# Turning the outputs of a down projection: 32x32 blocks on VectorE and 128-byte stores in place of TensorE transposes

## The chip, the cores and the metric

The kernel runs on one core of a Trainium2 chip. The metric is the time of one execution on the device in microseconds, as the median of several runs. The engines are named as in the profile: PE is TensorE's matmul, PEld its weight load, DVE is VectorE, ACT is ScalarE, POOL is GpSimd, SP is SyncE, which here does nothing but put DMA transfers into its queue. Transfers that ACT or POOL put into a queue stand as ACTq and POOLq.

## The reference

One layer of an encoder: 512 new frames of one stream and 64 frames of another, 2048 channels, all in f32. The part that matters here is the last one, the feed-forward block with its residual:

```python
h2 = rmsnorm(x, g_norm2)
x = x + (jax.nn.silu(h2 @ w_gate) * (h2 @ w_up)) @ w_down
```

with `w_gate`, `w_up` of 2048 x 5632 and `w_down` of 5632 x 2048. It gives `y_prompt` (512 x 2048) and `y_sample` (64 x 2048), both with the token as the row. Ahead of it stand the attention heads, the gated convolution and their joint projection, which the change does not touch.

## The kernel before

All activations lie with the channel on the partition and the token in the free dimension. The 512 and 64 tokens are taken together as 576 (T) and cut into two halves of 288 (HALF, HALVES); so the second half holds 224 tokens of the prompt and the 64 of the sample.

Each f32 operand is split into two parts of a rounded type, `hi` and `lo`, and a product is three matmuls (hi x hi, lo x hi, hi x lo), line 1529. The large products are cut in 2 x 2 blocks of channels and tokens and made by a scheme of seven block products in place of eight: sums of weight blocks are made on DVE (lines 1471 to 1477), split by ACT (line 221) and DVE (line 222), and each product (`run`, with a number 1 to 7) adds into one, two or more of the four quarters of the result.

The down projection works on eight column blocks d of 256 output columns. The list DOWN says in which order the blocks are visited and over which pairs of hidden channels; an entry is a unit. The last eight units are the last visits of the eight blocks: blocks 0, 1, 3, 6 and 7 with five pairs each, block 5 with six, and then blocks 2 and 4 with four. In a unit of m pairs each of the seven runs has 3m matmuls of 128x288. The runs of neighbouring units are interleaved: run 1 of the next unit comes before runs 3 and 4 of this one.

A block's result has four quarters `acc[d, c, i]`, with c one of two groups of 128 columns and i one of the two halves of tokens; each is a tile of 128 channels x 288 tokens, into which DVE (line 1559) and POOL (line 1561) add. The last visit finishes them in the order (0, 0), (1, 1), (0, 1), (1, 0); in the very last unit (1, 0) comes before (0, 1). When a quarter is finished, `store_y` (line 1685) spawns its output work in a pipeline.

The pipeline (`Pipeline`, lines 66 to 91) counts ticks, one for each pair in a product, that is every three matmuls. A piece of work says with `yield n` that its next step shall be given out n ticks later. In the last part of the kernel ACT, DVE, SP, POOL and PE all take their instructions in the order in which the program gives them out, so a step's place in each engine's queue is set by its ticks.

The output work of a quarter before the change has three steps. After 9 ticks (4 in the last unit, `quick`) PE transposes two pieces of 128 tokens against an identity matrix into PSUM (line 1717), and, where a rest of 32 or 64 tokens is due, a third piece (line 1720). For blocks 4 and 5 (`lone`) each quarter has a rest of 32 tokens; for the others the two halves of a column group lie in one tile (`both`), and the second of them turns the rests of both, 64 tokens. Three ticks later ACT copies the result from PSUM back over the tile (line 1723), and the rest into a spare part of `raw_b` (line 1727). Four ticks later SP stores it: rows of 128 columns, so pieces of 512 bytes, in one transfer for the first half (line 1730), in up to three for the second (lines 1697 and 1699, as prompt and sample are two outputs), and one or two for the rest. In the last unit the rests go out by ACT's queue. In the last unit there are no ticks between the steps.

In the same queue of SP, in program order, stand the loads of the down projection's weights (`load_columns`, line 1415), each given out when the buffer that it fills has been read for the last time. The last two of them are issued at 2330 us. The loads of the hidden activations (lines 1678 and 1685) are in this queue too; the last of them come before the first store.

Of the kernel before, what the change touches and what calls it, by code (L numbers as in the profile page):

```python
# [16 lines left out]
P = 128  # L17
TP = 512
TS = 64
T = TP + TS  # L20
HALF = T // 2
# [73 lines left out]
def tile_hybrid_stream_step(  # L95
# [6 lines left out]
    nc = tc.nc  # L102
# [5 lines left out]
    yp, ys = y_prompt[0], y_sample[0]  # L108
# [52 lines left out]
    def weight_raw(i):  # L161
        src, nk, ncol = specs[i]
        raw = raw_tile["A"][:, i % 2, : nk * ncol]
        return raw, raw.rearrange("p (k c) -> p k c", k=nk), src
# [64 lines left out]
    ident = const.tile([P, P], F32, name="ident")  # L229
# [29 lines left out]
    def misc(name):  # L259
        return ps_z.tile([P, 512], F32, tag="misc", name=name, bufs=2)  # L260

    rows = {}
# [109 lines left out]
    with tc.manual_schedule(engines={mybir.EngineType.Activation, mybir.EngineType.DVE, mybir.EngineType.SP}):  # L372
        raw, raw3, src = weight_raw(0)
# [106 lines left out]
    t1 = tc.alloc_tile_pool(name="t1", bufs=1, reuse_waits="tile", side="left")  # L480
    dg = t1.tile([P, 5, P], F32, tag="vtok", name="dg")
    for i in range(5):
        n = P if i < 4 else TS
# [690 lines left out]
    for k_, (n, p_) in enumerate(corder):  # L1174
# [7 lines left out]
        if n == NCU - 1 and p_ in (6, 7, 4):  # L1182
            q = {6: 1, 7: 2, 4: 3}[p_]
            t = bt["pool"].tile([P, NH, 2, HALF], F32R, tag=f"t{q}", name=f"forms{q}")
# [244 lines left out]
    late = {}  # L1429
# [16 lines left out]
    NU = len(UNITS)  # L1446
# [86 lines left out]
    def run(n, p_):  # L1533
# [8 lines left out]
        def done(c, i, ps, part=None):  # L1542
            if kind != "down":
                finish(kind, fp, c, i, ps, part)
            elif n in last:
                store_y(n, c, i)
# [68 lines left out]
    for d, v in visits.items():  # L1615
        n = next(a for a, b in zip(v, v[1:]) if a >= NGU + 10 and b >= a + 4)
# [3 lines left out]
    both, one = {}, {}  # L1620
    down = {}
    turn = [0]
# [64 lines left out]
    def store_y(n, c, i):  # L1687

        d = UNITS[n][1]
        src, cs, f0 = acc[d, c, i], slice((2 * d + c) * P, (2 * d + c + 1) * P), HALVES[i][0]  # L1690
        r = HALF - 2 * P

        def put(f, ap, q=nc.sync):

            rows, n_p = ap.shape[0], max(min(TP - f, ap.shape[0]), 0)
            if n_p:
                q.dma_start(out=yp[f : f + n_p, cs], in_=ap[:n_p])
            if n_p < rows:
                q.dma_start(out=ys[f + n_p - TP : f + rows - TP, cs], in_=ap[n_p:])

        quick = n == NU - 1


        lone = (d, c) not in both
        k0 = 0 if lone or i == 0 else r
        rest = None
        if lone:
            rest = src[:, 2 * P :], f0 + 2 * P
        elif (d, c) in one:
            rest = both[d, c].rearrange("p i t -> p (i t)")[:, 2 * P : 2 * P + 2 * r], 2 * P  # L1710
        one[d, c] = i

        def work():
            yield 4 if quick else 9
            po = misc("pot")[:, : 3 * P]
            for q in range(2):
                nc.tensor.transpose(po[:, q * P : (q + 1) * P], src[:, k0 + q * P : k0 + (q + 1) * P], ident)
            if rest:
                nr = rest[0].shape[1]
                nc.tensor.transpose(po[:nr, 2 * P :], rest[0], ident)  # L1720
            yield 0 if quick else 3
            ob = src[:, k0 : k0 + 2 * P].rearrange("p (i c) -> p i c", c=P)
            nc.scalar.copy(out=ob, in_=po[:, : 2 * P].rearrange("p (i c) -> p i c", c=P))
            if rest:
                turn[0] += 1
                obs = late["raw"][: 2 * r, 4096 + turn[0] % 4 * P : 4096 + (turn[0] % 4 + 1) * P]
                nc.scalar.copy(out=obs[:nr], in_=po[:nr, 2 * P :])
            yield 0 if quick else 4
            if i == 0:
                nc.sync.dma_start(out=yp[: 2 * P, cs].rearrange("(i p) c -> p i c", p=P), in_=ob)  # L1730
            else:
                put(f0 + k0, ob[:, 0, :])
                put(f0 + k0 + P, ob[:, 1, :])
            if rest:
                put(rest[1], obs[:nr], nc.scalar if quick else nc.sync)

        pipe.spawn(work())


# [105 lines left out]
```

## Time and profile before

| What | Value |
|---|---|
| time, median of 3 runs | 2382.36 us (2382.0 to 2385.2) |
| span of the profiled execution | 2383.4 us |
| PE busy | 2361.4 us (99%) |
| DVE busy | 1919.3 us (81%) |
| ACT busy | 1172.1 us (49%) |
| POOL busy | 295.2 us (12%) |
| DMA packets | 512,260, 390.76 MB, of them under 512 bytes 11,838 |
| stores of y | 80 by SP, 4 by ACT |
| first and last transposes for the outputs | 2267.7 and 2378.9 us |

The profile comes from one execution, whose span is 1.0 us above the median of the runs. The page gives the busy time of each engine, the share of time in 40 slices, the DMA queues, and the chain of waits that ended last. A row of a timeline gives the start in us, the length in us, the engine, the line of the kernel, the operation, the tile written and the tile read, and the number of instructions that were merged. A row of a group gives line, engine, operation, tiles, shapes and count, then the busy time in us, the mean of one in ns, and the idle time before with what ended it. A row of one line's or one tile's instructions gives the count and the shortest, the median and the longest duration in ns, and when the first and the last of them started. The time of a DMA row on SP is the time that the queue spends on issuing it, not the transfer's.

### The profile page before, as it was taken

Reading aid. Unit: us, or ns where it says so; the run is one execution under the profiler, and the core shown is the slowest. Engines: PE = TensorE matmul, PEld = TensorE weight load, DVE = VectorE, ACT = ScalarE, POOL = GpSimd, SP = SyncE. Lnnn points to the kernel's source line nnn. Section 1 sums busy time; section 2 is a strip of 40 time slices with the busy share of each in tenths; the row PEclk is TensorE's granted clock in tenths of the full one; section 3 lists DMA queues with packets and bytes.
Section 4 is the critical chain, followed back from the end, with each engine's and each line's share of the span. In section 5 each row is a group of like instructions: output and inputs, shape, how many; then the busy total and the mean of one; then the engine's idle time right before and its main releaser. Section 6 shows DMA issues by size and latency. Waiting matters only on the chain.

```text
span 2383.4 us, 44109 instructions
## 1 busy us (share of the span) xinstructions
PE 2361.4 (99%) x17765; PEld 2349.5 (99%) x17765; DVE 1919.3 (81%) x2884; ACT 1172.1 (49%) x2107; POOL 295.2 (12%) x386
## 2 busy tenths in 40 slices
PE   8999999999999999999999999999999999999999
PEld 8999999999999999999999999999999999999999
DVE  7767776688887899888888888888888777887876
ACT  6666665444444555444444444444444444444444
POOL 1111111242111130000000000000000002431211
PEclk9999999999999999999999999999999999999999
DMA  8354433584367745444444444444444936886642
GB/s 257 117 152 142 144 112 96 184 285 127 109 216 199 217 155 177 151 125 147 152 131 143 150 137 140 147 144 134 146 147 133 355 116 207 221 231 198 202 132 81
DMA packets 512260, 390.76 MB, mean 164 GB/s; under 512 B 11838, under 2 KB 501176, under 8 KB 512056
## 3 DMA queue, kind: packets, MB, share of 16 engines
q1 hardware_dynamic: 502712, 371.40, 48.8%
q0 software_dynamic: 8624, 16.22, 3.3%
q8 instruction: 139, 2.28, 0.4%
q14 instruction: 65, 0.53, 0.1%
q10 hardware_dynamic: 720, 0.33, 0.0%
HBM read 298.82 MB, written 89.08 MB: 163 GB/s over the span
## 4 chain that ended last, share of the span: by engine, by line
PE 88%; DVE 5%; DMA 3%; ACT 2%; issue 1%; POOL 0%; SPq 0%; ACTq 0%; DVEq 0%; POOLq 0%
PE psy L1529 34%; PE psw L1529 17%; PE pj L212 11%; PE psx L1529 9%; PE psy L1033 5%; PE pjo L212 4%; PE psw L1033 3%; PE psx L1033 1%; DMA raw_a<-in_w_out_dram 1%; DMA o_ob<-xt_dram 1%; DVE whl L1005 1%; PE z L682 1%; PE po L749 0%; DMA raw_a<-in_w_down_dram 0%; DMA raw_a<-in_w_in_dram 0%
## 5 line engine op out<-in xcount | busy, mean ns | idle before, releaser
L1529 PE MATMUL psy<-h_s,whl 128*128 128x288 f32 x2787 | 411.4, 294 | 0.3 <-ACT part L1539 0.3
L212 PE MATMUL pj<-x,whi 128*128 128x288 f32 x1856 | 398.2, 299 | 0.3 <-DVE x L355 0.3
L1529 PEld LDWEIGHTS psy<-h_s,whl 128*128 128x128 f32 x2787 | 383.5, 188 | 0.6 <-ACT part L1539 0.6
L222 DVE TENSOR_TENSOR whl<-raw_a,whl 128x1024 fp32r<-128x1024 f32 (+4 forms) x296 | 323.1, 1092 | 59.1 <-ACT whl L221 58.3
L1529 PE MATMUL psw<-t,whl 128*128 128x288 f32 x2400 | 348.1, 295 | 0.0
L1529 PEld LDWEIGHTS psw<-t,whl 128*128 128x128 f32 x2400 | 327.7, 188 | 0.0
L221 ACT CAST whl<-raw_a 128x1024 fp32r<-128x1024 f32 (+4 forms) x296 | 267.8, 906 | 114.5 <-issue 35.4
L212 PEld LDWEIGHTS pj<-x,whi 128*128 128x128 f32 x1856 | 306.6, 189 | 1.0 <-DVE x L355 0.6
L212 PE MATMUL pj<-x,wlo 128*128 128x288 f32 x928 | 274.2, 295 | 0.1
L222 DVE TENSOR_TENSOR whl<-raw_b,whl 128x1024 fp32r<-128x1024 f32 (+5 forms) x190 | 200.6, 1056 | 70.4 <-ACT whl L221 69.2
L221 ACT CAST whl<-raw_b 128x1024 fp32r<-128x1024 f32 (+5 forms) x190 | 165.2, 872 | 169.1 <-issue 72.8
L1539 ACT COPY part<-psy 128x288 f32<-128x288 f32 x242 | 96.4, 398 | 282.8 <-PE psy L1529 281.3
L1529 PE MATMUL psy<-b22m,whl 128*128 128x288 f32 x1212 | 182.7, 294 | 0.4 <-ACT part L1539 0.4
L1529 PE MATMUL psy<-t2t,whl 128*128 128x288 f32 x1212 | 183.0, 294 | 0.0
L212 PEld LDWEIGHTS pj<-x,wlo 128*128 128x128 f32 x928 | 174.9, 188 | 0.7 <-DVE wlo L422 0.3
L1529 PE MATMUL psx<-h_s,whl 128*128 128x288 f32 x1185 | 173.5, 294 | 0.0
L1529 PEld LDWEIGHTS psy<-b22m,whl 128*128 128x128 f32 x1212 | 168.0, 188 | 0.7 <-ACT part L1539 0.7
L1529 PEld LDWEIGHTS psy<-t2t,whl 128*128 128x128 f32 x1212 | 168.2, 188 | 0.2 <-DVE whl L222 0.2
L1529 PEld LDWEIGHTS psx<-h_s,whl 128*128 128x128 f32 x1185 | 162.6, 188 | 0.0
L221 ACT CAST whl<-s 128x1024 fp32r<-128x1024 f32 (+5 forms) x81 | 72.3, 892 | 101.5 <-PE psw L1529 101.4
L1308 POOL DMA_DIRECT2D hid_dram<-form x3 | 2.2, 750 | 947.2 <-DVE form L222 947.2
L1529 PE MATMUL psy<-t,whl 128*128 128x288 f32 x576 | 107.6, 296 | 0.0
(483 smaller groups left out, 4446.7 us busy)
## 6 DMA issues: line engine op xcount, KB each, us to landing
hid_dram<-form SPq DMA_DIRECT2D x147, 288.0 KB, 2.3
raw_a<-in_w_in_dram SPq DMA_DIRECT2D x41, 1024.0 KB, 6.5
raw_a<-in_w_gate_dram SPq DMA_DIRECT2D x22, 1024.0 KB, 6.0
raw_a<-in_w_up_dram SPq DMA_DIRECT2D x22, 1024.0 KB, 5.7
raw_b<-in_w_gate_dram SPq DMA_DIRECT2D x22, 1024.0 KB, 6.6
raw_b<-in_w_up_dram SPq DMA_DIRECT2D x22, 1024.0 KB, 7.6
h_s<-hid_dram SPq DMA_DIRECT2D x10, 2016.0 KB, 11.6
raw_a<-in_w_out_dram SPq DMA_DIRECT2D x16, 1024.0 KB, 5.4
```

Source lines behind the costliest of these rows:

```text
L212: mm(ps, w_[:, k, csl], x_, start=(k == 0 and n == 0), stop=(k == nk - 1 and n == 2))
L221: nc.scalar.copy(out=hi, in_=src)
L222: (lo_eng or nc.vector).tensor_tensor(out=lo, in0=src, in1=hi.bitcast(F32), op=ALU.subtract)
L682: mm(zb[i], a_[:, kk], b_[:, q0:TP], start=(n == 0), stop=False, skip_group_check=True)
L1005: tt(out=whl[:, 1], in0=src, in1=whl[:, 0].bitcast(F32), op=ALU.subtract)
L1033: mm(ps, whl[:, w_, j, :], x_, start=(start and j == 0 and q == 0), stop=(j == m - 1 and q == 2), skip_group_check=True)
L1308: q.dma_start(out=hid_dram[fp][2 * n - 2 : 2 * n].rearrange("f p t -> p f t"), in_=t.bitcast(F32))
L1529: mm(ps, whl[:, w_, j, :], x_, start=(start and j == 0 and q == 0), stop=(j == len(xs_) - 1 and q == 2), skip_group_check=True)
L1539: nc.scalar.copy(out=t, in_=st["y"])
```

## The change

The transposes on PE, their copies on ACT and the rests are gone. When a quarter is finished, DVE turns its tile in place: each block of 32 channels x 32 tokens is transposed by itself, so that afterwards partition 32q + t holds, at 32b + c, what partition 32q + c held at 32b + t. That is, of the tokens 32b + t for all b, the 32 channels of group q lie next to one another. A store then takes 32 partitions (one q), and writes for each partition t and each block b a piece of 32 channels, 128 bytes, to the row of token 32b + t. Nine blocks make up a half of 288 tokens; the second half is cut at token 512, into seven blocks for the prompt and two for the sample. The first step comes 9 ticks after the quarter is finished (4 in the last unit), the stores 2 ticks later, all of them on SP's queue.

```diff
         d = UNITS[n][1]
         src, cs, f0 = acc[d, c, i], slice((2 * d + c) * P, (2 * d + c + 1) * P), HALVES[i][0]
-        r = HALF - 2 * P
-        def put(f, ap, q=nc.sync):
-            rows, n_p = ap.shape[0], max(min(TP - f, ap.shape[0]), 0)
-            if n_p:
-                q.dma_start(out=yp[f : f + n_p, cs], in_=ap[:n_p])
-            if n_p < rows:
-                q.dma_start(out=ys[f + n_p - TP : f + rows - TP, cs], in_=ap[n_p:])
...
+        def put(f, ap):
+
+            n_p = max(min(TP - f, HALF), 0)
+            for y, t0, t1, g in ((yp, 0, n_p, f), (ys, n_p, HALF, f + n_p - TP)):
+                if t1 > t0:
+                    for q in range(4):
+                        nc.sync.dma_start(
+                            out=y[g : g + t1 - t0, cs.start + 32 * q : cs.start + 32 * (q + 1)].rearrange("(b t) c -> t b c", t=32),
+                            in_=ap[32 * q : 32 * (q + 1), t0:t1].rearrange("t (b c) -> t b c", c=32))
         def work():
-            yield 4 if quick else 9
-            po = misc("pot")[:, : 3 * P]
-            for q in range(2):
-                nc.tensor.transpose(po[:, q * P : (q + 1) * P], src[:, k0 + q * P : k0 + (q + 1) * P], ident)
-            if rest:
-                nr = rest[0].shape[1]
-                nc.tensor.transpose(po[:nr, 2 * P :], rest[0], ident)
-            yield 0 if quick else 3
-            ob = src[:, k0 : k0 + 2 * P].rearrange("p (i c) -> p i c", c=P)
-            nc.scalar.copy(out=ob, in_=po[:, : 2 * P].rearrange("p (i c) -> p i c", c=P))
...
-            yield 0 if quick else 4
-            if i == 0:
-                nc.sync.dma_start(out=yp[: 2 * P, cs].rearrange("(i p) c -> p i c", p=P), in_=ob)
-            else:
-                put(f0 + k0, ob[:, 0, :])
-                put(f0 + k0 + P, ob[:, 1, :])
-            if rest:
-                put(rest[1], obs[:nr], nc.scalar if quick else nc.sync)
+
+            yield 4 if n == NU - 1 else 9
+            nc.vector.transpose(out=src, in_=src)
+            yield 2
+            put(f0, src)
 
         pipe.spawn(work())
```

More of the change, by code (lines that the diff above doesn't have):

```diff
@@ L1690, in store_y @@
         src, cs, f0 = acc[d, c, i], slice((2 * d + c) * P, (2 * d + c + 1) * P), HALVES[i][0]
-        r = HALF - 2 * P
-        def put(f, ap, q=nc.sync):
-            rows, n_p = ap.shape[0], max(min(TP - f, ap.shape[0]), 0)
-            if n_p:
-                q.dma_start(out=yp[f : f + n_p, cs], in_=ap[:n_p])
-            if n_p < rows:
[L1699 to L1711, printed above, removed]
-        def work():
-            yield 4 if quick else 9
-            po = misc("pot")[:, : 3 * P]
-            for q in range(2):
-                nc.tensor.transpose(po[:, q * P : (q + 1) * P], src[:, k0 + q * P : k0 + (q + 1) * P], ident)
-            if rest:
-                nr = rest[0].shape[1]
-                nc.tensor.transpose(po[:nr, 2 * P :], rest[0], ident)
-            yield 0 if quick else 3
-            ob = src[:, k0 : k0 + 2 * P].rearrange("p (i c) -> p i c", c=P)
-            nc.scalar.copy(out=ob, in_=po[:, : 2 * P].rearrange("p (i c) -> p i c", c=P))
-            if rest:
-                turn[0] += 1
-                obs = late["raw"][: 2 * r, 4096 + turn[0] % 4 * P : 4096 + (turn[0] % 4 + 1) * P]
-                nc.scalar.copy(out=obs[:nr], in_=po[:nr, 2 * P :])
-            yield 0 if quick else 4
-            if i == 0:
-                nc.sync.dma_start(out=yp[: 2 * P, cs].rearrange("(i p) c -> p i c", p=P), in_=ob)
-            else:
-                put(f0 + k0, ob[:, 0, :])
-                put(f0 + k0 + P, ob[:, 1, :])
-            if rest:
-                put(rest[1], obs[:nr], nc.scalar if quick else nc.sync)
```

## The prediction

> **What bounds the kernel now.** I read the page first, then the busy times of the stretch in which outputs are stored, then the chain of waits of that stretch, then what SP's queue did there. The page:
>
> ```profile
> span 2383.4 us, 44109 instructions
> PE 2361.4 (99%) x17765; PEld 2349.5 (99%) x17765; DVE 1919.3 (81%) x2884; ACT 1172.1 (49%) x2107; POOL 295.2 (12%) x386
> ```
>
> TensorE (PE) works all the time, so what it no longer has to do shortens the span, as long as nothing else ends later. The stores fall in the last 122 us. Busy times there and in its middle (columns: length, then busy us of each engine, granted clock, share of the DMA engines, GB/s), and the shares of the chain of waits from 2262 us on:
>
> ```profile
> core 0: us, PE busy (x) PEld busy (x) DVE busy (x) ACT busy (x) POOL busy (x), PEclk, DMA share, GB/s
> 2262.00:2384.00 122.00, 116.58 (x887) 115.73 (x886) 84.14 (x117) 56.43 (x128) 20.51 (x24) 1.00 0.37 111
> 2282.00:2370.00 88.00, 88.00 (x674) 87.95 (x673) 63.74 (x89) 42.11 (x93) 13.88 (x17) 1.00 0.37 111
> ```
>
> ```profile
> by line: PE psy L1529 49.4%; PE psw L1529 25.0%; PE psx L1529 12.8%; PE pot L1717 5.5%; PE pot L1720 1.6%; issue 0.8%; ACT raw_b L1727 0.6%; ACT acc L1723 0.4%; ACT whl L221 0.4%; ACTq L1697 0.3%; ACT part L1539 0.0%; ACTq L1723 0.0%
> ```
>
> PE is busy 88.00 of 88 us: in this stretch it alone sets the pace, at the full clock. The transposes that the change removes (L1717, L1720) are 5.5% + 1.6% of the chain. DVE is free for 24 us of the 88. Now SP's queue in time (start, length, what); each row is the time that SP spends on putting a transfer into the queue, not the transfer:
>
> ```profile
> 2271.51 0.37 SPq L1415 DMA_DIRECT2D raw_a<-in_w_down_dram  x1
> 2314.87 0.40 SPq L1415 DMA_DIRECT2D raw_b<-in_w_down_dram  x1
> ...
> 2356.84 0.83 SPq L1697 DMA_DIRECT2D out_dram<-acc  x2
> 2357.72 0.42 SPq L1699 DMA_DIRECT2D out_dram<-acc  x1
> 2358.24 0.37 SPq L1699 DMA_DIRECT2D out_dram<-raw_b  x1
> ...
> 2371.78 0.38 SPq L1730 DMA_DIRECT2D out_dram<-acc  x1
> 2372.26 0.94 SPq L1697 DMA_DIRECT2D out_dram<-acc  x2
> 2373.25 0.59 SPq L1699 DMA_DIRECT2D out_dram<-acc  x1
> 2373.88 0.59 SPq L1697 DMA_DIRECT2D out_dram<-raw_b  x1
> 2374.57 0.53 SPq L1730 DMA_DIRECT2D out_dram<-acc  x1
> 2375.20 0.47 SPq L1697 DMA_DIRECT2D out_dram<-raw_b  x1
> ...
> 2379.77 0.83 SPq L1697 DMA_DIRECT2D out_dram<-acc  x2
> 2380.64 0.42 SPq L1699 DMA_DIRECT2D out_dram<-acc  x1
> ```
>
> SP issues one transfer after the other. Back to back, seven stores take 2371.78 to 2375.67, 0.56 us each; the four from 2356.84 take 1.77 us, 0.44 each. The issue does not follow the bytes: a weight load of more than a megabyte (L1415) costs 0.37 to 0.40 us, a store of 32 rows 0.37. So the number of stores counts, not their size. The end of the work:
>
> ```profile
> 2377.47 0.57 PE L1529 MATMUL psy<-h_s,whl 128*128 128x288 f32 x3
> 2378.07 0.46 DVE L1559 TENSOR_TENSOR acc<-psy,acc 128x288 f32<-128x288 f32 x1 [1.42 <-PE psy L1529]
> ```
>
> The last product ends at 2378.04, the span 5.4 us later; from the end of the last issue (2380.64 + 0.42 = 2381.06) to the end of the span it is 2.3 us.
>
> **Part 1, removed from PE and ACT.** Thirty-two calls of the store (8 column blocks, 4 quarters each) make 2 transposes each, and 20 of them a third for the rest: 84 transposes. The chain gives their price in time (start, length), and the matmuls of a tick beside it:
>
> ```profile
> 2351.59 0.22 PE pot L1717 x2
> 2360.77 4.00 PE psy L1529 x30
> 2365.56 0.22 PE pot L1717 x2
> 2376.48 0.22 PE pot L1717 x2
> ```
>
> A transpose is 0.11 us of PE's time, a pipeline tick (three matmuls) 0.40. 84 x 0.11 = 9.2 us; the shares of the chain above, 7.1% of the 121.4 us to the end, give 8.6, the difference being the transposes after the last product. I take 8.6 as PE's gain. ACT loses 52 copies, which no one waited for but the transposes and stores themselves; I count nothing for it but the 0.6 us that PE waits near 2371 for such copies. PE would end at 2378.0 - 8.6 - 0.6 = 2368.8.
>
> **Part 2, added on DVE.** 32 transposes of 128x288. No row shows this operation; the nearest is the addition of the same shape:
>
> ```profile
> L1559 DVE TENSOR_TENSOR acc<-psw,acc 128x288 f32<-128x288 f32 x11 | 5.0, 454 | 6.0 <-PE psw L1529 6.0
> ```
>
> Lower end 0 (an operation cannot take less), upper end two such passes, 0.9 us; I take 0.45, as one operand is read where the addition reads two and elements are put out at the same count. 32 x 0.45 = 14.5 us, of it some 24 x 0.45 = 11 us in the stretch of 88 us where DVE is free for 24. So it hides there, at no cost. Behind a waiting transpose stand DVE's weight splits, for which PE waits; but the transpose comes 9 ticks (3.6 us) after the block's last addition, so it waits for nothing. In the last unit it is 4 ticks, 1.6 us.
>
> **Part 3, added on SP.** Each of the 16 column groups gets 4 stores for the first half of the tokens (one for each 32 channels) and 8 for the second half, which is cut at token 512: 16 x 12 = 192 stores, in place of 84. Nearest rows for the issue of one (operation, count, shortest/median/longest ns):
>
> ```profile
> L1697 SPq DMA_DIRECT2D out_dram<-raw_b x14: 416/530/644, 2280.9 to 2375.2; - x14
> L1699 SPq DMA_DIRECT2D out_dram<-acc x10: 417/587/596, 2321.4 to 2380.6; - x10
> L1699 SPq DMA_DIRECT2D out_dram<-raw_b x2: 365/366/366, 2354.5 to 2358.2; - x2
> ```
>
> The new stores carry 36, 28 or 8 KB from 32 partitions. Nearest by size are the stores of raw_b, mostly 32 KB: 0.53 us, and 0.05 from the end of one to the start of the next (2371.78 + 0.38 = 2372.16 is followed at 2372.26, 2372.26 + 0.94 at 2373.25): 0.58 us per store, which is near the train of seven (0.56). Ends: 0.37, the shortest row, with no gap; 0.65, the longest of the usual rows with its gap.
>
> What this does to the end: a unit of five pairs makes 24 stores, 24 x 0.58 = 13.9 us and one load of 0.4. Seven runs of five ticks are 14.0 us of PE without transposes. So SP just keeps up, late by half a us more in each unit; in the last two units (four pairs, 11.2 us) it falls behind. The stores are now issued 2 ticks after the turn, where before 7 ticks passed. The train that ends last begins with the second quarter of the sixth block to finish, transposed at 2351.59 before. By then 50 of the 84 transposes have gone, 5.5 us; two ticks add 0.8: 2346.9. From there 68 stores follow (20 to finish that block, 24 and 24), with no pause, as each later quarter is ready before SP comes to it. 68 x 0.58 = 39.4: 2386.3; with the 2.3 us after the last issue the span ends at 2388.6.
>
> The same from the start of the stretch, as a check on the ends of the price. The first store was made ready by the transpose at
>
> ```profile
> L1717 PE MATMUL pot<-ident,acc_z x12: 270/272/273, 2267.7 to 2308.4; 128*128 128x128 f32 x12
> ```
>
> so SP can begin at 2268.5. 192 stores and 6 loads of 0.45, and some 2.9 us in which SP waits for the second quarter: at 0.58 it is 2385.5 for the last issue (less than 2386.3, as there are more pauses), at 0.65 it is 2398.9 and the span 2401.2. At 0.44, SP catches up until the last two units: from the quarter at 2365.56 (less 7.0, plus 0.8: 2359.4) 44 x 0.44 = 19.4, span 2381.1. At 0.37 only the last 20 stores count, from 2376.48 - 8.9 + 0.8 = 2368.4: 2375.8, span 2378.1. The gain of PE is gone at about 0.50 us per store.
>
> **Part 4, loads behind stores.** The weight loads of the next units are in the same queue. How much time they have:
>
> ```profile
> 2323.63 0.84 ACT L221 CAST whl<-raw_b 128x768 fp32r<-128x768 f32 x1 [1.21 <-PE psx L1529]
> DMA to landing us min/median/max: 6.1/6.4/7.0
> SPq L1415 <- DVE whl L222: 23.9, 5, 11.4
> ```
>
> The load issued at 2314.87 lands some 6.4 us later and is first read at 2323.63: 2.4 us to spare. And SP waits for DVE before each load (23.9 us over 5), so a train late by less than that delays no load. At 0.58 the lateness stays under 3 us: nothing. At 0.65 it comes to 8 us at the last load, and PE waits, but then SP is the later of the two anyway.
>
> **Part 5, pieces of 128 bytes.** 576 tokens x 2048 columns in runs of 32 elements are 36,864 pieces in place of 9,216 of 512 bytes. No row has pieces of 128 bytes. The DMA queue of a stretch of stores alone (2352 to 2366), and of loads (2160 to 2200; packets, MB, share of 16 engines' time):
>
> ```profile
> q1 hardware_dynamic: 1296, 0.57, 14.9%
> q1 hardware_dynamic: 8524, 9.13, 70.2%
> ```
>
> 14.9% of 14 us x 16 is 33.4 us for 1,296 packets: 26 ns each, at 440 bytes on the mean. The loads: 449 us for 8,524 packets, 53 ns at 1,071 bytes. A line through the two gives 43 ns per KB and 7 ns fixed: 12.5 ns at 128 bytes. Ends: 7 ns (the fixed part) and 26 ns (no gain by being small). The largest stores have 288 pieces, 18 for each of 16 engines, 0.13 to 0.47 us, below SP's 0.58 in any case. I take 12.5 ns and count nothing.
>
> The row first, then the rule: the Trainium skill, "DMA: Bandwidth & Descriptors", section Specifications, says that under 512 bytes a DMA engine reads, changes and writes, and so falls from line rate. No run here shows it. By that rule a piece would cost two passes, an estimate of 52 ns, 0.94 us for a store of 288 pieces, and the span would be that of rival (b) at this price, 2415.
>
> **Sum.** 2388.6 against 2383.4 of the same profiled execution: +5.2. The median of the runs is 2382.4, 1.0 under that span; so 2387.6 us.
>
> **Rivals.** (a) *SP keeps up, and PE's gain stays.* It needs 0.50 us per store or less. For it: the four stores at 0.44, and the 32-row rows of 0.37. Against it: 0.53 and 0.59 for 32 KB. The span is 2378 to 2384, by the ends above; at 0.37 the time is 2377.1. It ends on the other side below 0.50.
> (b) *The DMA engines, not SP, are slow with 128-byte pieces.* A unit has 4,608 pieces, 288 for each engine, and a load of 80 pieces of 1 KB, 4 us; in 14 us there is room for 10/288 = 35 ns per piece. Above that the queue fills, SP is held, loads land late and PE waits. At 52 ns the 36,864 pieces take 120 us of the 16 engines and six loads 24: from 2268.5, with 2.3 at the end, the span is 2415. For it: nothing in the traces has pieces so small; against it: the time per packet goes with the bytes (26 and 53 ns). 60 ns would give 2268.5 + 138 + 24 + 2.3 = 2433.
> (c) *DVE is late.* If a turn takes 0.9 us, 24 of them are 22 of DVE's 24 free us; each split then comes up to 0.9 late, and PE, which waits for splits, loses at most what a turn takes over 0.45: 30 x 0.45 = 13 us. PE then ends near 2382, the last 12 stores take 7 us, and the span is near 2391.
>
> **How the numbers follow.** The forecast case (0.50 to 0.65 us per store, 2384 to 2401 of span): 0.42, of it 0.14 within 0.2% of before and 0.28 slower. (a) 0.27: 0.14 within, 0.13 faster by over 0.2%. (b) 0.25, all slower. (c) 0.06, 0.05 of it slower, 0.01 within. Within 0.2% (4.8 us) is about what a measurement of this kernel cannot tell from no change. Faster 0.13, same 0.29, slower 0.58. The range goes from 2376 (past the lower end of (a) little is left, under one in ten) to 2436, which takes in (b) up to 60 ns; about one in ten lies above. The forecast case alone is 2383 to 2400.
>
> **What would show it.** SP's rows of the new stores: about 0.53 us each with gaps of 0.05, in trains without a pause from the second half of the stretch on, and the chain of waits ending in SP's queue for some 20 us instead of in PE. PE's last product near 2368.8. DVE's turn at 0.45 us, and no new wait of PE for a split. The mean time of a packet of the stores falls to near 12 ns. The prediction is wrong if a store's issue is under 0.5 or over 0.65 us, if packets of 128 bytes take over 35 ns, or if loads land so late that PE stops.

## The result, and the profile after

The changed kernel takes 2389.5 us, the median of 10 runs (2387.4 to 2393.5), against 2385.1 us of the kernel before on the same chip (10 runs, 2382.0 to 2387.5): a ratio of 1.0021 with a 95% interval of 1.0012 to 1.0030. It is slower by 0.2%, near the limit of what can be told from no change, and 1.9 us above the predicted 2387.6. The profiled execution is the longest of the ten, 2393.5 us.

The page:

```profile
span 2391.8 us, 43988 instructions
PE 2353.4 (98%) x17681; PEld 2342.1 (98%) x17681; DVE 1931.7 (81%) x2916; ACT 1159.9 (48%) x2055; POOL 299.4 (13%) x386
```

PE has 84 instructions less and 8.0 us less to do, yet the span is 8.4 us longer. So time in which PE does nothing has come in. The busy times of the same stretch, of the kernel before and then of the changed one (columns as in the prediction):

```profile
2262.00:2364.00 102.00, 102.00 (x779) 101.95 (x779) 76.72 (x105) 49.91 (x109) 18.11 (x21) 1.00 0.40 122
```

```profile
2262.00:2364.00 102.00, 98.60 (x739) 97.67 (x738) 89.84 (x134) 42.29 (x72) 23.78 (x22) 1.00 0.50 122
```

Before, PE did not stop in these 102 us; now it stops for 3.4. What SP's queue did over the whole stretch after the change (start, length, what):

```profile
2273.66 0.37 SPq L1415 DMA_DIRECT2D raw_a<-in_w_down_dram  x1
2274.09 13.73 SPq L1698 DMA_DIRECT2D out_dram<-acc_z  x24
2287.93 0.40 SPq L1415 DMA_DIRECT2D raw_b<-in_w_down_dram  x1
...
2304.62 0.40 SPq L1415 DMA_DIRECT2D raw_a<-in_w_down_dram  x1
2305.07 2.69 SPq L1698 DMA_DIRECT2D out_dram<-acc_z  x4
2307.86 6.95 SPq L1698 DMA_DIRECT2D out_dram<-acc_ax  x8
2314.91 3.73 SPq L1698 DMA_DIRECT2D out_dram<-acc_z  x8
2318.74 1.86 SPq L1698 DMA_DIRECT2D out_dram<-acc_ax  x4
2320.70 0.40 SPq L1415 DMA_DIRECT2D raw_b<-in_w_down_dram  x1
...
2337.54 51.71 SPq L1698 DMA_DIRECT2D out_dram<-acc  x96
```

From 2287.93 on SP hardly rests. Between the load at 2304.62 and the next one at 2320.70 it issues 24 stores, and these take all of the 16.1 us, 0.67 us each: the last twelve go at 0.47 (3.73 / 8 and 1.86 / 4), the twelve right behind the load at 0.81 (from 2305.07 to 2314.81). These twelve are not alike. SP's own waits over the whole stretch, and the row of 2307.86 as two narrower timelines cut it:

```profile
SPq L1698 <- DMA raw_a<-in_w_down_dram: 2.5, 3, 0.9
SPq L1698 <- DMA raw_b<-in_w_down_dram: 1.9, 2, 1.0
```

```profile
2307.86 3.80 SPq L1698 DMA_DIRECT2D out_dram<-acc_ax  x3
...
2312.59 2.21 SPq L1698 DMA_DIRECT2D out_dram<-acc_ax  x5
```

The first seven take 6.6 us from 2305.07 on, 0.94 each. Then SP waits 0.9 us until the load has landed, and the next five take 0.44 each. This wait comes once for each of the five times that SP loads in the stretch, and each time it is the eighth transfer behind a load that waits. In the trace the transfers of SP report their landing on eight semaphores in turn, so the eighth needs the one that the load still holds.

At the end stands a train of 96 stores. Its last 75, from a timeline that begins at 2352, and the last work of the other engines:

```profile
2351.83 37.43 SPq L1698 DMA_DIRECT2D out_dram<-acc  x75
```

```profile
2373.61 0.56 PE L1529 MATMUL psy<-h_s,whl 128*128 128x288 f32 x3
2374.21 0.46 DVE L1559 TENSOR_TENSOR acc<-psy,acc 128x288 f32<-128x288 f32 x1 [0.67 <-PE psy L1529]
```

37.43 / 75 is 0.50 us each. PE's last product ends at 2374.2 and SP's last issue at 2389.26: for 15 us only stores go out. The span ends 2.5 us later.

Why PE stops is in the waits of the stretch (engine, line, what it waited for: us in total, times, longest), and in the order of things around one such stop:

```profile
ACT whl L221 <- DMA raw_a<-in_w_down_dram: 10.8, 3, 6.0
ACT whl L221 <- DMA raw_b<-in_w_down_dram: 9.2, 2, 4.9
...
PE psy L1529 <- ACT part L1539: 3.1, 3, 1.9
```

```profile
2312.68 0.72 ACT L221 CAST whl<-raw_a 128x640 fp32r<-128x640 f32 x1 [5.96 <-DMA raw_a<-in_w_down_dram]
2313.30 0.39 ACT L1539 COPY part<-psy 128x288 f32<-128x288 f32 x1
...
2313.75 0.67 PE L1529 MATMUL psy<-t,whl 128*128 128x288 f32 x3 [1.90 <-ACT part L1539]
```

ACT waits 6 us for the weights that SP asked for at 2304.62. Behind that cast in ACT's queue stands a copy out of PSUM (line 1539), and PE waits for this copy. Before the change, these waits for loads are not among the rows of the stretch at all. The new parts themselves (a line's instructions: count, shortest, median and longest ns; the DMA queue in 2346 to 2386, where only stores are in it: packets, MB, share of 16 engines):

```profile
L1705 DVE STREAM_TRANSPOSE acc<-acc x20: 430/468/474, 2317.4 to 2375.0; 128x288 f32<-128x288 f32 x20
```

```profile
L1698 SPq DMA_DIRECT2D out_dram<-acc x120: 316/444/1342, 2321.1 to 2388.8; - x120
```

```profile
q1 hardware_dynamic: 16307, 1.93, 31.0%
```

A turn is 0.468 us. An issue is mostly 0.44 us, but up to 1.3. A packet takes 0.31 x 40 us x 16 / 16,307 = 12.2 ns.

Executions reach this stretch at times that differ by some microseconds. So below, moments are counted from the issue of the load of raw_b that precedes it, which in the kernel before and the changed one is

```profile
2259.61 0.37 SPq L1415 DMA_DIRECT2D raw_b<-in_w_down_dram  x1
```

```profile
2261.41 0.37 SPq L1415 DMA_DIRECT2D raw_b<-in_w_down_dram  x1
```

By this count PE's last product ends at +118.4 before and +112.8 after, SP's last issue at +121.4 and +127.8, the span at +123.8 and +130.4. The change costs 6.6 us in these two executions, 4.4 by the medians.

### The profile page after: what moved, and what is told of

It is laid out like the page before. It is cut to its first block, busy times and chain, and to the rows that moved or that the text cites. A ratio compares the mean times of both kernels' runs of the same rounds, so it can differ in the third digit from the quotient of the medians.

```text
span 2391.8 us, 43988 instructions
## 1 busy us (share of the span) xinstructions
PE 2353.4 (98%) x17681; PEld 2342.1 (98%) x17681; DVE 1931.7 (81%) x2916; ACT 1159.9 (48%) x2055; POOL 299.4 (13%) x386
## 4 chain that ended last, share of the span: by engine, by line
PE 81%; DVE 9%; DMA 4%; ACT 3%; issue 2%; POOL 1%; SPq 1%; DVEq 0%; ACTq 0%; POOLq 0%
PE psy L1529 33%; PE psw L1529 16%; PE pj L212 10%; PE psx L1529 8%; PE psy L1033 6%; PE psw L1033 3%; PE psx L1033 1%; DMA raw_b<-in_w_down_dram 1%; DVE wlo L175 1%; DVE whl L222 1%; DMA o_ob<-xt_dram 1%; DMA raw_a<-in_w_down_dram 1%; DMA raw_a<-in_w_out_dram 1%; PE pjo L212 1%; DVE po L1216 0%
```

## The experiments

My theory after the result: PE's gain is real, but the end is now set by SP, which has too many stores to issue; and the loads, which stand in the same queue, come late. The rivals: that the pieces of 128 bytes are what costs, in the DMA engines; and that DVE or ACT hold PE up. In the table, ratios are to the kernel before on the same chip, and moments are in us from that load of raw_b, in the profiled execution.

| Kernel | stores of y | ratio (95%) | PE's last product | SP's last issue | span |
|---|---|---|---|---|---|
| before | 84 | 1 | +118.4 | +121.4 | +123.8 |
| changed | 192 | 1.0021 (1.0012 to 1.0030) | +112.8 | +127.8 | +130.4 |
| a quarter of the stores | 48 | 0.9957 (0.9945 to 0.9970) | +108.8 | +111.0 | +113.5 |
| pieces of 512 bytes | 192 | 1.0005 (0.9996 to 1.0014) | +108.8 | +121.6 | +124.2 |
| 64 pieces per store | 192 | 1.0001 (0.9992 to 1.0010) | +108.7 | +121.0 | +123.5 |
| before, pieces of 128 bytes | 100 | 1.0005 (0.9996 to 1.0013) | +118.4 | +121.9 | +124.2 |
| two queues | 192 | 1.0045 (1.0032 to 1.0057) | +126.6 | +130.8 | +133.6 |
| loads on POOL | 192 | 1.0093 (1.0077 to 1.0108) | no such load on SP | | |
| halves merged | 144 | 1.0006 (0.9997 to 1.0014) | +109.3 | +122.8 | +125.3 |
| halves merged, tail on two queues | 144 | 1.0034 (1.0021 to 1.0046) | +109.5 | +129.1 | +131.6 |
| five blocks turned by DVE | 114 | 0.9977 (0.9968 to 0.9986) | +113.4 | +116.4 | +118.9 |
| six blocks turned by DVE | 120 | 0.9993 (0.9984 to 1.0002) | +112.0 | +119.0 | +122.0 |

### A quarter of the stores

```diff
-                    for q in range(4):
+                    for q in range(1):
```

> The changed kernel with only the first of the four channel groups stored (48 stores in place of 192; three quarters of y are left out). Theory: without the train the span ends some 5 us after PE, which ends near 2369: 0.4% under before. Rival (DVE's turns hold PE): PE ends near 2374 as in the changed kernel, 0.2% under before at most. This is also the most that any way of storing can give.

Measured: 0.9957. The turns on DVE are all there, and 48 stores. The same stretch, and what becomes of the tail of SP's queue:

```profile
2262.00:2364.00 102.00, 102.00 (x772) 101.88 (x772) 91.31 (x141) 43.45 (x74) 24.49 (x24) 1.00 0.31 89
```

```profile
2325.30 43.29 SPq L1698 DMA_DIRECT2D out_dram<-acc  x24
```

PE does not stop, although DVE is busy for 91.31 of the 102 us against 76.72 before. PE's last product comes 9.6 us earlier than before (+118.4 to +108.8). So the transposes were worth what they cost, and neither DVE's turns nor ACT take it back. All that the changed kernel loses lies in the stores: 113.5 against 130.4, 16.9 us.

### The number of stores and the number of pieces

Two kernels keep the 192 stores and change what each carries. In the first a store has 64, 32 or 16 rows of 512 bytes in place of 288, 224 or 64 pieces of 128:

```diff
-                            out=y[g : g + t1 - t0, cs.start + 32 * q : cs.start + 32 * (q + 1)].rearrange("(b t) c -> t b c", t=32),
-                            in_=ap[32 * q : 32 * (q + 1), t0:t1].rearrange("t (b c) -> t b c", c=32))
+                            out=y[g + 32 * nb * q : g + 32 * nb * (q + 1), cs].rearrange("(b t) c -> t b c", t=32),
+                            in_=ap[32 * q : 32 * (q + 1), t0 : t0 + P * nb].rearrange("t (b c) -> t b c", c=P))
...
```

> The changed kernel with as many stores (192) from the same 32 partitions, but in pieces of 512 bytes: each store writes whole rows of 128 columns, so the values land in wrong places and part of the rows is left out (2 of 2.25 pieces per partition in the first half, 1 in the second, 16 partitions for the samples). Theory (the number of stores counts): as the changed kernel, 0.1 to 0.3% over before, SP's train ending near 2389. Rival (pieces of 128 bytes are what costs): the train gets shorter and the time falls under before by 0.2% or more.

In the second a store keeps pieces of 128 bytes but has 64 of them each time:

```diff
-                            in_=ap[32 * q : 32 * (q + 1), t0:t1].rearrange("t (b c) -> t b c", c=32))
+                            in_=ap[32 * q : 32 * (q + 1), t0 : t0 + 64].rearrange("t (b c) -> t b c", c=32))
```

> The changed kernel with its 192 stores in place, each cut to its first two blocks of 32 tokens: 64 pieces of 128 bytes in place of 288, 224 or 64 (two thirds of y are left out). Theory (issues count, pieces hold them only behind a load): as the run with pieces of 512 bytes, some 6 us under the changed kernel, within 0.1% of before. Rival (the cost lies in the pieces alone): as the run with a quarter of the stores, 0.4% under before.

Measured: 1.0005, a little under what I expected, with SP's train ending 6 us sooner than in the changed kernel, where I expected it to end as late; and 1.0001, as expected. The stretch in the first and in the second, and SP's queue in the second:

```profile
2262.00:2364.00 102.00, 102.00 (x773) 101.86 (x772) 90.48 (x140) 43.33 (x74) 26.21 (x24) 1.00 0.36 106
```

```profile
2262.00:2364.00 102.00, 102.00 (x772) 101.86 (x771) 90.44 (x140) 43.53 (x74) 25.34 (x24) 1.00 0.33 90
```

```profile
2297.15 0.40 SPq L1415 DMA_DIRECT2D raw_a<-in_w_down_dram  x1
2297.60 2.15 SPq L1698 DMA_DIRECT2D out_dram<-acc_z  x4
2300.09 5.45 SPq L1698 DMA_DIRECT2D out_dram<-acc_ax  x8
...
2327.30 50.72 SPq L1698 DMA_DIRECT2D out_dram<-acc  x96
```

PE keeps its whole gain in both (102.00 of 102 us busy, +108.8 and +108.7). The span is as before the change, although SP still has 192 stores. So the 144 stores that the quarter leaves out cost 10.0 us at the end (113.5 to 123.5) nearly by their number alone: the second kernel has 12,288 pieces in all, the one with a quarter of the stores 9,216. Their price is not the issue alone. With 64 pieces per store SP also waits 8.7 us, in six waits, for loads to land, each time with the eighth transfer behind one; with a quarter of the stores no such wait is among SP's rows, as only six stores stand between two loads. The last train of 96 is nearly as long as in the changed kernel, 50.7 against 51.7 us: over the whole train the price of a store hardly depends on what it carries. But it begins 5.9 us earlier (2327.30 is +70.3; 2337.54 is +76.1). This is the second part, 6.9 us from +123.5 to +130.4 in these executions and 4.8 us by the ratios (1.0021 against 1.0001; the profiled execution of the changed kernel is its longest): with full pieces SP comes out of every unit later. The eight stores of acc_ax, the fifth to the twelfth behind a load, take 5.45 us here and 6.95 in the changed kernel. Two things differ: with full pieces the seven issues behind a load are longer (6.6 us from 2305.07 on, against 3.7 from 2297.60 on here), and the load takes longer to land (where the profile gives the time, up to 8.6 us against up to 6.0 here). That the issue is held until pieces of the load and of the stores ahead have left the queue is how I read it; no row shows the queue's filling.

### Pieces of 128 bytes in the kernel before

```diff
+        def small(y):
+            return y[:, 2 * d * P : (2 * d + 2) * P].rearrange("p (g h c) -> p h g c", h=2, c=32)[:, c]
-                q.dma_start(out=yp[f : f + n_p, cs], in_=ap[:n_p])
+                q.dma_start(out=small(yp[f : f + n_p]), in_=ap[:n_p].rearrange("p (g c) -> p g c", c=32))
...
```

> The kernel before, with its transposes on PE, but its stores cut into pieces of 128 bytes (32 columns at a step of 64 over the block's 256 columns, so the columns land in wrong places); the store of 256 rows becomes two, 100 stores in place of 84. Theory: within 0.1% of before, as 16 issues of 0.4 us find room in SP's queue. Rival (pieces of 128 bytes fill the DMA engines): 36,864 pieces here too, so as slow as the changed kernel or more, 0.2% or more over before.

Measured: 1.0005, PE's last product and SP's last issue within 0.5 us of before. The pieces alone cost nothing that can be measured where SP has time between the stores. In these runs they cost only together with the number of stores.

### Two queues

```diff
-                        nc.sync.dma_start(
+                        (nc.scalar if q % 2 else nc.sync).dma_start(
```

> The changed kernel with the stores of two of the four channel groups put into ACT's queue in place of SP's; nothing else differs. Theory (SP's train of stores paces the end): SP has 96 stores, some 50 us of issue in the 120 us, is never late, loads come back to their old places, PE keeps its 9 us and its last product ends near 2370; time 0.3 to 0.4% under the kernel before. Rival (the 16 DMA engines are what 128-byte pieces fill): the same pieces on the same engines, so 0.2% over before, as the changed kernel. Rival (DVE's turns hold PE): PE's last product stays near 2374, 0 to -0.2%.

Measured: 1.0045, slower than the changed kernel, where I expected a gain. Waits of the stretch:

```profile
ACT part L1539 <- DMA out_dram<-acc: 13.6, 4, 5.6
...
PE psy L1529 <- ACT part L1539: 9.9, 7, 3.7
```

ACT's queue is on PE's path: its copies out of PSUM stand behind the stores that it now issues, and these wait for earlier stores. PE ends 14 us later than in the changed kernel. The theory of SP's load is not touched by this, but the remedy is wrong. The Trainium skill, "DMA: Bandwidth & Descriptors", section Issuing engines are not separate DMA queues, says that a second issuing engine saves only the time on the sequencer, usually small beside the transfer. In the changed kernel's trace that time is indeed the smaller, 0.44 us against 1.6 us from issue to landing, and yet it is what limits. Here the second engine gives none of it back, because of the work that stands behind the issue on that engine.

### Loads on POOL

The last six weight loads leave SP's queue and go, each in two transfers, through POOL.

```diff
-            nc.sync.dma_start(out=t.rearrange("p (k e) -> p k e", e=wide_),
+            cuts = (0, m, 2 * m) if n >= NU - 6 else (0, 2 * m)
+            for k0, k1 in zip(cuts, cuts[1:]):
+                (nc.gpsimd if n >= NU - 6 else nc.sync).dma_start(
+                    out=t.rearrange("p (k e) -> p k e", e=wide_)[:, k0:k1],
...
```

> The changed kernel with the last six weight loads put into POOL's queue, each in two parts (12 transfers), in place of SP's; stores and all else as in the changed kernel. Theory (loads behind stores cost PE 4 us, and stores behind a load are held in SP's queue, which makes a store 0.54 us on the mean where it is 0.49 elsewhere): PE's last product comes 4 us earlier than in the changed kernel, SP's train is about 192 x 0.49 = 94 us of issue and keeps up until the last two units, and the time is 0.2 to 0.3% under the changed kernel, so 0.1% under before to no change. Rival (what holds PE is not the loads' place in SP's queue): PE ends as in the changed kernel and the time stays 0.2% over before.

Measured: 1.0093, a miss. Waits (lines 1532 and 1564 here are 1529 and 1561 of the other kernels):

```profile
POOL raw_a L1417 <- issue: 19.5, 5, 4.6
...
DVE acc L1708 <- POOL acc L1564: 15.9, 2, 11.2
PE psw L1532 <- DVE whl L222: 15.8, 5, 8.5
```

Up to 4.6 us pass on POOL at a load of raw_a, up to 4.9 at one of raw_b, in which it waits for nothing that the profile shows. These seven waits all lie between two halves that POOL issues one right after the other, and each ends 0.3 us after the first of the two has landed: the halves issued at 2305.99 and 2323.25 land after 5.2 and 5.4 us, and the next ones begin at 2311.46 and 2328.97. So it looks like a wait for the half before, which a load in one transfer may not have; no run here tries that. Its additions stand behind that, DVE's turn waits for the addition, the weight split stands behind the turn in DVE's queue, and PE waits for the split. So this says nothing on late loads. But it says something on stores with full pieces and no load in their own queue:

```profile
2313.72 3.69 SPq L1701 DMA_DIRECT2D out_dram<-acc_ax  x8
```

These are 0.46 us each, although until about 2316.2 the half issued at 2311.46 is on its way through POOL's queue, and the DMA engines are busy for 0.85 of the time (2313.7 to 2316.2). That speaks for the shared queue, and against busy DMA engines, as what holds the stores behind a load in the changed kernel. It is no full proof, as a transfer here is half as large as a load there. The run also shows the wait that the prediction looked for and did not find in the change itself: a turn that is late does hold up PE.

### Halves merged

A group of 128 columns is stored when both halves are turned, where they lie in one tile: 8 stores in place of 12, the same pieces.

```diff
...
-            put(f0, src)
+            if whole:
+                put(0, both[d, c].rearrange("p i t -> p (i t)"))
+            elif not pair:
+                put(f0, src)
```

> The changed kernel, but where the two halves of a column group lie in one tile (six of eight blocks) each half is turned as before and both are stored together once the second has been turned: 8 stores (4 of 16 blocks of prompt tokens, 4 of the samples) in place of 12; 144 stores in all, the same 36,864 pieces. Theory (the number of stores paces the end): the train shrinks by 48 x 0.54 = 26 us, SP keeps up but for the last unit, whose last 12 stores follow PE's end: 12 x 0.49 + 0.9 + 2.3 = 9 us after a last product 9 us earlier than before; 0.15 to 0.3% under before. Rival (the pieces fill the DMA engines): as many pieces, so 0.1% over before or more.

Measured: 1.0006, a miss: 0.15% under the changed kernel by the two ratios, but no gain over before. PE has its gain (+109.3). The tail is still SP's:

```profile
2338.38 45.72 SPq L1703 DMA_DIRECT2D out_dram<-acc  x80
```

Eighty stores, 0.57 us each with the waits for turns among them, end 13.5 us after PE. In the last three units fewer stores also begin later, as each waits for the second half.

### Halves merged, the tail on two queues

The same, and in the last unit the odd q of two quarters go through ACT.

```diff
+        split_queues = n == NU - 1 and (c, i) in ((1, 0), (0, 1))
...
-                        nc.sync.dma_start(
+                        (nc.scalar if split_queues and q % 2 else nc.sync).dma_start(
```

> As the kernel with merged stores, and in the last unit the stores of the last two quarters are shared between SP's and ACT's queues (ACT has no cast or copy left then). Theory: the 12 stores after PE's end take 3 us in place of 6, so another 0.1% off: 0.3 to 0.4% under before. Rival (ACT's queue shares what holds the stores, as when half of all stores went there): no better than the merged kernel.

Measured: 1.0034, a miss. PE is not held up this time (+109.5), but SP is: the waits of SP and the two queues:

```profile
SPq L1705 <- DMA out_dram<-acc: 13.4, 2, 13.2
```

```profile
2369.22 2.84 ACTq L1705 DMA_DIRECT2D out_dram<-acc  x6
2370.89 16.96 SPq L1705 DMA_DIRECT2D out_dram<-acc  x34
```

SP, with 34 stores still to issue, stands still for 13.2 us, until 1.7 us after ACT has issued its first. In the trace the stores of both queues report their landing on the same eight semaphores, and the one that SP waits for there is that of ACT's first store, which ACT could not issue before its turn was done; no run here takes this wait alone away. Either way a second queue did not shorten the first one's backlog: it stopped it.

### Five blocks, six blocks

If the end is lost to SP's tail alone, then DVE should turn the blocks for which SP has time, and PE the last ones. In the kernel before, blocks 0, 1, 3, 6 and 7 are turned by DVE and stored with merged halves; blocks 5, 2 and 4 stay as they were. The second version has NU - 1 in the condition, so that DVE turns block 2 too.

```diff
...
+        if not lone and n < NU - 2:
+            pipe.spawn(work_turned())
+            return
```

> The kernel before, but the five blocks 0, 1, 3, 6 and 7 are turned by VectorE and stored as in the experiment with merged halves (8 stores for each group of 128 columns, pieces of 128 bytes); blocks 5, 2 and 4, the last three, keep TensorE's transposes and their 512-byte stores. 50 of the 84 transposes go: 50 x 0.11 = 5.5 us of PE. My account (the end is lost to SP's train of stores behind the last products, and only there; the pieces cost when a load stands behind them): 80 new stores over five units of 14 us are 16 in a unit, 16 x 0.57 = 9.1 us, so SP keeps up and the end is as before, some 3 us behind PE: PE's last product 4 to 5.5 us earlier against the load ahead of the stretch (+113 to +114.5, span +118.5 to +120), ratio to the kernel before 0.9977 to 0.9985. Rival (the loads behind pieces of 128 bytes land late whatever the number of stores, and PE loses at them what the transposes gave): PE's last product at +117 or later, ratio 0.9995 to 1.0005.

> The same with block 2, the last but one, turned by VectorE too: only blocks 5 and 4 keep TensorE's transposes. 60 transposes go, 6.6 us of PE. Block 2's 16 stores of 128-byte pieces (0.57 each, 9.1 us) fall into the last unit, 11.2 us of PE, beside block 5's and 4's: my account gives an end of SP no more than 1 to 3 us later than in the experiment with five blocks against PE's last product; ratio to the kernel before 0.9974 to 0.9988, within 0.1% of that experiment. The rival of late loads gives 0.9995 to 1.0005 here too.

Measured: 0.9977 with five blocks, 0.9993 with six. The first is faster than both kernels: 2380.5 us against 2386.1 before (11 and 21 runs), and 0.44% under the changed kernel by the two ratios (0.9977 / 1.0021). Everything of it came within what my account gave: PE's last product at +113.4, the span at +118.9. SP's queue with five blocks, and its busy row:

```profile
2322.73 8.92 SPq L1717 DMA_DIRECT2D out_dram<-acc  x16
2331.75 1.03 SPq L1415 DMA_DIRECT2D raw_a<-in_w_down_dram  x2
2337.86 8.81 SPq L1717 DMA_DIRECT2D out_dram<-acc  x16
...
2376.27 0.42 SPq L1699 DMA_DIRECT2D out_dram<-acc  x1
```

```profile
2262.00:2364.00 102.00, 101.09 (x764) 100.64 (x763) 88.03 (x133) 44.72 (x84) 22.31 (x21) 1.00 0.48 124
```

Sixteen stores of a block take 9 us of a unit's 14, and SP waits for work again. PE stops for 0.9 us in place of 3.4. With six blocks the forecast missed: the ratio lies above its range and just under that of the rival. But the rival, by which PE loses at late loads what the transposes gave, is not what came, as PE's last product is at +112.0. The span ends 5.5 us behind PE's last product with five blocks and 10 with six, SP's last issue 3 and 7 us behind, where I allowed 3 more. SP waits for the turn of block 2's second half, and then has everything of the last two units before it:

```profile
SPq L1717 <- DVE acc L1723: 8.4, 1, 8.4
```

```profile
2369.95 3.95 SPq L1717 DMA_DIRECT2D out_dram<-acc  x8
2373.99 0.40 SPq L1749 DMA_DIRECT2D out_dram<-acc  x1
2374.49 5.32 SPq L1717 DMA_DIRECT2D out_dram<-acc  x8
```

## Why the prediction came out right, point by point

The time was right within 2 us and the side as well, but that is in part luck: two errors inside the sum cancel, and one part failed. Two of the prediction's own signs of being wrong came true, an issue under 0.5 us (0.44 in the median) and loads so late that PE stops.

**Part 1 held.** PE's gain was taken as 9.2 us (8.6 for the transposes, 0.6 for a wait for their copies); without the stores in its way it is 9.6 (a quarter of the stores). In the changed kernel only 5.6 of it are left (+118.4 to +112.8); what took the rest is Part 4.

**Part 2 held.** A turn takes 0.468 us, not 0.45, and DVE hides it: in three kernels with all 32 turns PE is busy for 102.00 of 102 us. Rival (c) falls.

**Part 3, the sum right, the terms not.** The forecast was 68 stores from 2346.9 at 0.58 us, to 2386.3. By the timeline the last 75 take 0.50 each and end at 2389.26; so the last 68 begin near 2351.8 + 7 x 0.5 = 2355.3. This execution is 1.8 us behind that of before when the stretch begins, so the train started 6.6 us too late by the forecast, and was 68 x 0.08 = 5.4 us shorter. What was wrong with the start is, first, that the first store stands in SP's queue behind the load at 2273.66, which waits for DVE: 2274.1, not 2268.5, of which 1.8 is the execution's. (The turn itself begins only at 2272.1, as DVE has other work before it.) Second, a unit's 24 stores and their load were taken as 13.9 + 0.4 us, and take 16.1 from 2304.62 to 2320.70. The price of a store is not one number: 0.47 to 0.50 in a free queue, 0.94 for the seven behind the load at 2304.62, and then a wait until the load has landed. A single mean of 0.58 happens to lie between (2274.09 to 2389.26 is 115.2 us for 192 stores and five loads, 0.59 each).

Rival (a) had its condition met, 0.50 us per store in the tail, and did not come to pass, as SP entered the tail late. The chain of waits was to end in SP's queue for some 20 us; the view ends at DVE at 2375 and does not follow the stores, so the 15 us have to be read from SP's timeline.

**Part 4 failed.** It counted nothing, as SP's lateness would stay under 3 us and was covered by the wait for DVE before each load. The loads are issued at +26.5, +43.2, +59.3 and +75.1, against +25.0, +40.1, +55.3 and +70.5 before; and PE, without transposes, would like them sooner, at +24.9, +38.5, +52.4 and +66.6, as the kernel with a quarter of the stores has them. So the lateness grows to 8.4 us at the last, and the loads take longer to land, up to 8.6 us against 7.0 before. The cover was worked out from PE's old pace, which the change itself takes away. ACT waits 20 us for five loads, PE loses 3.4 of its 102 us. In this kernel that alone doesn't set the end, since SP is later still: as the prediction said for its upper price. But loads and stores hold each other up, through the one queue.

**Part 5, the price right, the conclusion not.** A packet takes 12.2 ns where 12.5 was taken. The rule of the Trainium skill ("DMA: Bandwidth & Descriptors", section Specifications), that below 512 bytes the engine reads, changes and writes, does not show as a second pass: 12.2 ns at 118 bytes on the mean and the 26 ns at 440 before lie on the prediction's line of 43 ns per KB and 7 ns fixed. So rival (b) falls as it was put, though what it said would follow, SP held, loads late and PE waiting, came at 12.2 ns where it needed more than 35. And "count nothing" is wrong by the step from 64 pieces per store to full ones, 4.8 us by the ratios and 6.9 in the profiled executions. The part set the engines' time of a store against SP's time for it, and not against the load that the engines carry at the same moment. The seven stores behind the load at 2304.62 have 4 x 288 + 3 x 224 pieces, 1.4 us of the 16 engines at 12.2 ns; with 64 pieces each it would be 0.3. By this estimate the load lands about 1 us later. The rest I put down to the stores that are held in SP's queue behind a load, which is argued from the run with loads on POOL and not isolated by a run.

In short, against +5.2 of the forecast, by the ratios: 10 us gained by PE (0.9957), 10.5 given back by the number of stores in SP's queue (to 1.0001), and 5 more by their pieces and the loads among them (to 1.0021). The last term was put at nothing, and the price of a store in the tail was put too high by about as much.

## What to carry to other kernels

A store costs its queue about half a microsecond whatever it carries, so a layout that cuts one store into four moves work from the tensor engine to the issuing queue; where that queue also holds the loads, count its time per unit of work against the new, faster pace and not against the old, and look how many transfers can go out behind a load before one has to wait for its landing (here seven). Use a cheaper path only as long as its queue drains: here turning five of eight blocks on VectorE was worth 0.23%, and turning all of them cost 0.21%. Before moving transfers to a second queue, look at what stands behind them on that engine, and who waits for it.

## What the runs showed of the hardware that I had not expected

The issue of a store lasts longer right behind a load in the same queue: mostly 0.44 us, but 0.94 on the mean over the seven stores behind one load of 1.25 MB, and 2.2 us in the longest case. The eighth transfer behind each load waited until the load had landed. A load given to POOL in two halves held that engine for up to 4.9 us between them, against 0.4 us for a whole load on SP. And a queue with a backlog can be stopped by another engine's queue: 13.2 us in the kernel with the tail on two queues.
